# Samples' output totals three chunks behind their sums, their recurrent reads with 128 weight columns, and factors of the last stage fetched in other iterations

## The chip, the core and the metric

The kernel runs on one core of one Trainium2 chip. The metric is the device time of one execution in microseconds (us). TensorE is called PE here, its weight loads PEld, VectorE DVE, ScalarE ACT, GpSimd POOL, and the queue from which most DMAs are issued is SyncE's, SP.

## What is computed

One inference step of a decoder with two layers, for a prompt of 2048 tokens and for 8 samples of 4 tokens each (32 rows), with the same weights. Layer 0 is gated linear attention with a recurrent state (4 heads of 128 x 512), layer 1 is sliding-window attention with sinks (32 heads of 64, 4 groups). The reference, cut to what matters:

```python
def gla_mixer(h, state0, norm_g, w_in, w_gate2, b_gate, out_norm_g, w_out):
    u = rmsnorm(h, norm_g)
    q, k, v, gate, g_low = jnp.split(u @ w_in, [...], axis=-1)
    log_a = jax.nn.log_sigmoid((g_low @ w_gate2 + b_gate).astype(jnp.float32)) / A_GATE_NORMALIZER
    o, state = gla_recurrence(heads(q, A_HEAD_DK) * (A_HEAD_DK ** -0.5), heads(k, A_HEAD_DK),
                              heads(v, A_HEAD_DV), heads(log_a, A_HEAD_DK), state0)
    o = rmsnorm(o, out_norm_g).reshape(bsz, seq_len, BRANCH_WIDTH)
    return (o * jax.nn.silu(gate)) @ w_out, state
...
    # one step of the recurrence, for a chunk; b is the running sum of log_a
    out = (jnp.einsum('bhtd,bhdv->bhtv', qc * jnp.exp(b), state)
           + jnp.einsum('bhts,bhsv->bhtv', scores, vc))
    new_state = (jnp.exp(b_last[:, :, 0, :, None]) * state
                 + jnp.einsum('bhsd,bhsv->bhdv', kc * jnp.exp(b_last - b), vc))
...
hp, hs = hp + gla_mixer(hp, zeros, *w), hs + gla_mixer(hs, state_gla, *w)    # layer 0
k_p, v_p = shared_kv(hp, ...); k_n, v_n = shared_kv(hs, ...)                 # one K/V for both groups
q_p, g_p = swa_query(hp, ...); q_s, g_s = swa_query(hs, ...)                 # layer 1
hp = hp + (swa_banded(q_p, k_p, v_p, sinks) * jax.nn.silu(g_p)) @ w_out
hs = hs + (attend(q_s, cache + k_n, cache + v_n, ..., sinks) * jax.nn.silu(g_s)) @ w_out
```

## The kernel before

Each float32 operand is split into a high and a low half-precision part, and a product is made of three passes, (high, high), (high, low) and (low, high). The prompt is cut into 16 chunks of 128 rows. Program order, priorities and waits are turned into each engine's order by a scheduler; from `pin[0] = True` on (stage 3 below) PE's order is kept as it is written.

**Stage 1, the heads of layer 0** (to about 1250 us). For each of 4 heads and 4 blocks of 512 rows the kernel projects, makes scores by levels, and runs the recurrence chunk by chunk. After a head's last block the samples follow (`SampleA.steps`): `mid` makes `Sh` (scores, 96 x 32) and `qm` (tile name `qe`), the decayed queries of 32 rows, once for each of the 8 samples and zero outside that sample's 4 rows. `seq(b)` reads one sample's old state: three matmuls add `qm[:, a, b, :]` (weights, 128 x 32) times the state's halves `sh` (tile `pst`) to the bank `po` (tile `o`, 32 rows), and one matmul `kv<-ke,skn` with 96 x 128 weights makes the state's update. These are woven into the next block's work on PE.

**Stage 2, the output of layer 0** (about 1150 to 1530 us). `a_out(c)` handles chunk c: `load` fetches four transposed tiles from DRAM (`sg` or `v`, in turn, one set for odd and one for even chunks), then two halves of 48 matmuls, in the banks `pj` and `o`, two buffers each. `fin` adds the residual on DVE (`E<-pj,X` and `st<-o,X`), stores it (`hd`), and norms and transposes it for layer 1. The load of chunk c+1 stands in the program ahead of chunk c. Woven between the matmuls are steps of `prep`, which splits the weights of layer 1: `form_steps` loads four tiles of `b_w_out` (`wraw`, `qT`, `kT`), subtracts on POOL (`sth`), splits on ACT and DVE, and stores (`wf`). After chunk 7 comes the samples' output: `out_sample` runs 128 small matmuls for each half (bank `lev`, then bank `kv`; weights are the columns of `wo` and `wo1`, the moving operand is `ogTs`), and its last step, `fin`, totals on ACT and DVE (`total`, tile `ssg`), transposes on PE (`tr<-idf,ssg`), adds the residual, and after the second half norms.

**Stage 3, layer 1** (about 1530 to 2590 us). 64 blocks (4 groups of 16 chunks) and three iterations more, n from 0 to 66, TOT being 64. Iteration n projects block n (`f` steps, 24 in an iteration), makes the scores of block n-2 (`A`) and the values of block n-3 (`B`): probabilities are split (`v`), transposed by DMA (`sth<-v`, `pst<-v`), and used as weights in `kv<-rmask,sth`. In iterations 64 to 66 the `f` steps are the first products of stage 4 and the samples' output `s_out(0)`.

**Stage 4, the output of layer 1** (to the end). Two chunks (a `Pair`) are multiplied with a fast form of seven products instead of eight, `PRODS`, with factors `wf0` to `wf6`. `Pair.load` fetches transposed attention outputs (`oge`); `Pair.sums` makes on DVE and ACT the sums that are some products' other operand. For the first pair these run within stage 3: `trickle` issues loads, `summing` makes the sums, one at every sixth `f` step.

## Time and profile before

| what | us |
|---|---|
| median of 3 runs | 2882.5 |
| lowest and highest | 2880.64, 2883.82 |
| the profiled execution | 2877.55 |
| its span, first to last instruction | 2875.8 |
| PE busy (95% of the span) | 2735.2 |
| DVE, ACT, POOL busy | 1850.9, 1441.6, 1062.2 |

The profiled execution lies 4.95 us under the median, and 1.75 us of it are outside the span. Engines work side by side; a stretch of time is saved only where the engine that all others wait for is waiting or busy for nothing. A wait is put down to what ended it. A row of the timeline merges neighbours of one kind: its second number is the time from the first one's start to the last one's end, so a row's start plus the others' spacing gives the start of its last instruction.

### The profile page before, as it was taken

The numbers are of one execution on the slowest core, as the hardware profiler recorded it, in microseconds if no ns is written. First come the engines' busy times: TensorE is split into PE (matmuls) and PEld (weight loads), VectorE is DVE, ScalarE is ACT, GpSimd is POOL, SyncE is SP. The second block draws the span as 40 slices with busy tenths as digits, with TensorE's granted clock in tenths as the row PEclk, the third lists the DMA queues.
The fourth block names the chain that finished last, engine by engine and source line by source line (L and its number), as shares of the span: only waits on it lengthen the run. The fifth ranks groups of instructions, "written<-read, shape, count | busy, mean of one in ns | idle before, by whom it ended". The sixth has DMA issues, their size and how long they took to land. (4 is left out here: it accounts for less than half of the span.)

```text
span 2875.8 us, 51606 instructions
## 1 busy us (share of the span) xinstructions
PE 2735.2 (95%) x19070; PEld 1386.7 (48%) x19070; DVE 1850.9 (64%) x3815; ACT 1441.6 (50%) x3385; POOL 1062.2 (37%) x1463
## 2 busy tenths in 40 slices
PE   6899999999999999996999999999999999989999
PEld 4445444444454444443444555555555554554444
DVE  5767787677768775336412666677767766767653
ACT  6655665465546554333312555566666656641110
POOL 1242233222322321126404686666557547530000
PEclk9999999999999999998999999999999999999999
DMA  8351334124312533799976566867767788798651
GB/s 211 86 124 36 99 94 155 38 81 136 114 38 88 166 85 96 182 240 275 234 161 159 104 130 123 205 113 133 171 113 132 151 146 164 153 232 180 134 113 56
DMA packets 774230, 391.78 MB, mean 136 GB/s; under 512 B 629200, under 2 KB 698776, under 8 KB 773944
## 3 DMA queue, kind: packets, MB, share of 16 engines
q1 hardware_dynamic: 761016, 352.75, 54.4%
q0 software_dynamic: 10880, 35.66, 3.5%
q8 instruction: 149, 2.44, 0.4%
q14 instruction: 105, 0.86, 0.1%
q10 hardware_dynamic: 2080, 0.07, 0.0%
HBM read 138.90 MB, written 107.54 MB: 86 GB/s over the span
## 5 line engine op out<-in xcount | busy, mean ns | idle before, releaser
L101 PE MATMUL pj<-W,uT 128*128 128x512 f16 x5088 | 1202.0, 382 | 5.9 <-ACT qT L430 2.5
L101 PEld LDWEIGHTS <-uT 128*128 128x128 f16 x6976 | 653.3, 98 | 716.1 <-issue 42.0
L101 PE MATMUL tr<-W,uT 128*128 128x512 f16 x1536 | 365.5, 379 | 0.0
L186 POOL TENSOR_SCALAR rs_m<-ss 128x1 f32<-128x1 f32 (+3 forms) x190 | 45.7, 241 | 702.8 <-ACT og L611 246.5
L101 PEld LDWEIGHTS <-X 128*128 128x128 f16 x2744 | 185.1, 98 | 155.3 <-issue 23.4
L1273 ACT ACTIVATE o<-o,mx 128x256 f32<-128x256 f32 (+1 forms) x384 | 168.6, 439 | 181.2 <-DVE mx L1268 171.9
L1268 DVE CUSTOM_DVE_ANT_0 o<-o,madd,nsink 128x256 f32<-128x256 f32 (+1 forms) x384 | 183.8, 479 | 47.3 <-PE o L101 42.5
L101 PE MATMUL pj<-uT,W 128*128 128x512 f16 (+1 forms) x912 | 186.8, 356 | 26.8 <-DMA uT<-ogT 23.4
L198 DVE SCALAR_TENSOR_TENSOR v<-o,v 128x512 f16<-128x512 f32 (+1 forms) x192 | 128.9, 671 | 107.0 <-ACT v L197 87.1
L187 POOL TENSOR_TENSOR rs_r<-rs_m,mhalf 128x1 f32<-128x1 f32 (+2 forms) x186 | 184.5, 992 | 14.4
L101 PEld LDWEIGHTS <-W 128*128 128x128 f16 x2448 | 129.9, 99 | 112.7 <-issue 17.7
L101 PEld LDWEIGHTS <-v 128*128 128x128 f16 x976 | 94.7, 98 | 115.4 <-issue 2.6
L508 POOL TENSOR_TENSOR E<-bt 128x256 f32<-128x256 f32 x96 | 73.2, 763 | 197.6 <-DVE X L195 118.3
L195 POOL TENSOR_TENSOR ogT<-og,ogT 128x512 f16<-128x512 f32 x68 | 88.2, 1297 | 153.2 <-ACT ogT L194 148.7
L101 PEld LDWEIGHTS <-sth 128*128 128x128 f16 x2080 | 110.0, 98 | 53.8 <-DMA sth<-v 14.0
L101 PE MATMUL o<-gl,X 128*128 128x256 f16 (+1 forms) x768 | 114.6, 272 | 12.6 <-DMA X<-qe 7.2
L101 PEld LDWEIGHTS <-sg 128*128 128x128 f16 x800 | 77.8, 98 | 94.0 <-issue 1.7
L101 PE MATMUL kv<-rmask,sth 128*128 128x64 f16 x1984 | 105.7, 193 | 11.4 <-DMA sth<-v 10.5
L197 ACT ACTIVATE v<-o 128x512 f16<-128x512 f32 (+1 forms) x192 | 111.3, 580 | 10.0 <-DMA sth<-v 6.5
L1273 ACT ACTIVATE lev<-lev,mx 128x256 f32<-128x256 f32 (+1 forms) x128 | 56.5, 442 | 105.0 <-DVE mx L1268 102.9
L101 PE MATMUL kv<-rmask,pst 128*128 128x64 f16 x992 | 100.8, 193 | 7.0 <-DMA pst<-v 7.0
L195 DVE TENSOR_TENSOR X<-E,X 128x512 f16<-128x512 f32 x128 | 95.6, 747 | 13.4 <-ACT X L194 13.1
(464 smaller groups left out, 5093.6 us busy)
## 6 DMA issues: line engine op xcount, KB each, us to landing
pre<-pst POOLq DMA_DIRECT2D x72, 256.0 KB, 3.6
W<-pre SPq DMA_DIRECT2D x36, 512.0 KB, 6.8
ogd<-ogT SPq DMA_DIRECT2D x68, 256.0 KB, 2.5
wraw<-in_a_w_in_dram SPq DMA_DIRECT2D x64, 256.0 KB, 2.8
wraw<-in_b_w_in_dram SPq DMA_DIRECT2D x64, 256.0 KB, 3.6
oge<-ogT SPq DMA_DIRECT2D x64, 256.0 KB, 2.9
wraw<-in_a_w_out_dram SPq DMA_DIRECT2D x32, 256.0 KB, 3.1
X<-in_x_prompt_dram SPq DMA_DIRECT2D x32, 256.0 KB, 3.2
```

The lines of the kernel that those rows point to most:

```text
L101: return order(nc.tensor.matmul(*a, **k))
L186: pool.tensor_scalar(m[:n, :k], ss, a, b, ALU.mult, ALU.add)
L187: pool.tensor_tensor(r[:n, :k], m[:n, :k], mhalf[:n, :k], ALU.pow)
L195: eng.tensor_tensor(lo, src, hi, ALU.subtract)
L197: act(hi, src, AF.Copy, scale=sc)
L198: dve.scalar_tensor_tensor(lo, src, sc, hi, ALU.mult, ALU.subtract)
L508: pool.tensor_tensor(Ev[:, :, 0, :], ref, btv[:, :, 0, :], ALU.subtract)
L1268: dve.tensor_tensor_reduce(pm[:, z], pm[:, z], madd.rearrange("p a b -> p (a b)")[:, (2 - nk) * P :], -0.125, nsink[:, g * GRP + h : g * G ...
L1273: act(pm[:, z], pm[:, z], AF.Exp, scale=-1.0, bias=nm_[:, h : h + 1], accum_out=bx["sum"][:, h : h + 1])
```

## The change

It has three parts. (1) `out_sample`'s matmuls stay behind chunk 7, both halves in a row, and the last steps (totals, transposes, residual, norm) are called behind chunk 10; the second half's total has a tile of its own (`sqk`). (2) `Sh` becomes 96 x 128 and `qm` gets three more blocks of 32 columns, both filled with zeros by POOL; `seq(b)` reads 128 columns, blocks b to b+3, and `po` has 128 rows, of which the first 32 are used. (3) `Pair.sums` of pair 0 is ordered with its step `four` last and begins half an iteration earlier, and four fetches are called in other iterations.

```diff
--- before.py
+++ after.py
@@ -733,9 +733,10 @@
             def mid():
                 bt, S = bx["bt"], bx["S"]
                 qs, ks = self.qkv[:, 0, :], self.qkv[:, 1, :]
-                Sh = bx["Sh"] = T("Sh", [96, SMP], F16, NG)
-                act(Sh, S, AF.Copy, scale=SST / (SQ * SQ))
-                dve.scalar_tensor_tensor(Sh[32:64], S[32:64], SST / (SQ * SQ), Sh[32:64], ALU.mult, ALU.subtract)
+                Sh = bx["Sh"] = T("Sh", [96, P], F16, NG)
+                pool.memset(Sh[:, SMP:], 0.0)
+                act(Sh[:, :SMP], S, AF.Copy, scale=SST / (SQ * SQ))
+                dve.scalar_tensor_tensor(Sh[32:64, :SMP], S[32:64], SST / (SQ * SQ), Sh[32:64, :SMP], ALU.mult, ALU.subtract)
                 E0 = T("k1", [P, SMP], F32, 2)
                 act(E0, bt, AF.Exp, scale=1.0 / 16)
                 ebl = bx["ebl"] = T("ebs", [P, NS], F32, 1)
@@ -743,9 +744,10 @@
                 dve.tensor_tensor(E0, E0, qs, ALU.mult)
                 qe = T("k2", [P, 2, SMP], F16, 2)
                 split((qe[:, 0], qe[:, 1]), E0)
-                qm = bx["qm"] = T("qe", [P, 2, NS, SMP], F16, NG)
+                qm = bx["qm"] = T("qe", [P, 2, NS + 3, SMP], F16, NG)
+                pool.memset(qm[:, :, NS:], 0.0)
                 for a in range(2):
-                    dve.tensor_tensor(qm[:, a], qe[:, a].unsqueeze(1).to_broadcast([P, NS, SMP]), bmq, ALU.mult)
+                    dve.tensor_tensor(qm[:, a, :NS], qe[:, a].unsqueeze(1).to_broadcast([P, NS, SMP]), bmq, ALU.mult)
 
             def stack():
                 bt = bx["bt"]
@@ -770,7 +772,7 @@
                 vst = bx["vst"] = T("ke", [96, 512], F16, NG)
                 act(vst, pv_, AF.Copy)
                 dve.tensor_tensor(vst[64:96], pv_[64:96], vst[64:96], ALU.subtract)
-                bx["po"] = PT("o", [SMP, 512], bufs=2)
+                bx["po"] = PT("o", [P, 512], bufs=2)
                 mm(bx["po"], bx["Sh"], vst, start=True, stop=False)
 
             def seq(b):
@@ -785,7 +787,7 @@
                 sh = T("pst", [P, 2, 512], F16, 2)
                 split((sh[:, 0], sh[:, 1]), sr, SST)
                 for n, (a, z) in enumerate(PASSES):
-                    mm(bx["po"], bx["qm"][:, a, b, :], sh[:, z], start=False, stop=b == NS - 1 and n == 2)
+                    mm(bx["po"], bx["qm"][:, a, b : b + 4, :].rearrange("p b t -> p (b t)"), sh[:, z], start=False, stop=b == NS - 1 and n == 2)
                 km = T("skn", [96, P], F16, 2)
                 dve.tensor_scalar(km, bx["kst"], bm[:, b : b + 1], None, ALU.mult)
                 pkv = PT("kv", [P, 512])
@@ -798,7 +800,7 @@
                     nc.sync.dma_start(o["st_s"][0, b - 1 : b + 1, h].rearrange("b p v -> p b v"), bx["sr"])
 
             def fin():
-                po = bx["po"]
+                po = bx["po"][:SMP]
                 ob = T("pst", [SMP, 512], F32, 2)
                 ss = T("ss", [P, 3], F32, 4)
                 act(ob, po, AF.Square, accum_out=ss[:SMP, 0:1])
@@ -1085,7 +1087,7 @@
         st, total = sproj_steps(tiles, len(kts or range(16)), lambda: ogTs[0], kts, (("lev", "kv")[half], 1))
 
         def fin():
-            t = T("ssg", [P, 4, SMP], F32, 1)
+            t = T(("ssg", "sqk")[half], [P, 4, SMP], F32, 1)
             total(t, 0, 4, sc)
             pt = PT("tr", [SMP, 512], bufs=2)
             for x in range(4):
@@ -1121,8 +1123,12 @@
         aout[c + 1][0]()
         weave(aout[c][1][0] + aout[c][1][1], some(each))
         if c == 7:
-            for half, w in enumerate((wo, wo1)):
-                run(out_sample(w.cols(4), half, a_finish_s))
+            late_s = [out_sample(w.cols(4), half, a_finish_s) for half, w in enumerate((wo, wo1))]
+            for st in late_s:
+                run(st[:-1])
+        if c == 10:
+            for st in late_s:
+                st[-1]()
 
 
     def rope_mul(eng, t1, t2, src, ct, st):
@@ -1604,7 +1610,7 @@
                 put(5, z, a[1, z])
 
             if self.p == 0:
-                return [lambda f=f, z=z: f(z) for z in range(2) for f in (one, two, three, four)]
+                return [lambda f=f, z=z: f(z) for z in range(2) for f in (one, two, three)] + [lambda z=z: four(z) for z in range(2)]
             return [lambda f=f, z=z: f(z) for f in (one, two, three, four) for z in range(2)]
 
         def add(self, tag, pp, t):
@@ -1707,28 +1713,28 @@
                     trickle.pop(0)()
                 if boundary and seen == 7 and n > TOT - NCH + 3:
                     boundary.pop(0)()
-                if summing and seen % 6 == 3:
+                if summing and seen % 6 == 3 and (n > TOT or seen > 12):
                     summing.pop(0)()
             elif lists[x]:
                 lists[x].pop(0)()
         if n < NKV * NCH and c == 12:
             if g + 1 < NKV:
                 run(gw[g + 1].steps())
-        if n == TOT - 8:
+        if n == TOT - 11:
             t_ = T("uT", [P, 8, 8, P], F16, 4)
             for x in range(4):
                 pr = pairs[x // 2]
                 pr.l[x % 2] = [t_[:, 2 * x], t_[:, 2 * x + 1]]
                 pr.fetch(x % 2, pr.l[x % 2])
-        if n in (TOT - 6, TOT - 3):
-            run(quarters(wform_big, {TOT - 6: 0, TOT - 3: 2}[n]))
-        if n == TOT - 4:
+        if n in (TOT - 7, TOT - 3):
+            run(quarters(wform_big, {TOT - 7: 0, TOT - 3: 2}[n]))
+        if n == TOT - 14:
             run(quarters(wform, 3))
         if n == TOT - 1:
             trickle += [lambda x=x: pairs[0].load(x) for x in (3, 2, 0, 1)] + quarters(wform_big, 1)
+            summing += pairs[0].sums()
         if n == TOT:
             trickle += quarters(wform, 4) + quarters(wform, 5)
-            summing += pairs[0].sums()
         if n == TOT + 1:
             trickle += quarters(wform_big, 6)
         if boundary:
```

What the scheduler makes of it, as built. **PE in stage 2**, around the samples' output: `kv` is the bank of the second half's sums, `tr<-idf,ssg` and `tr<-idf,sqk` are the transposes of the totals, `W` weights. Before:

```order
L101 MATMUL kv_14338<-ogTs_3953,uT_11567 128x64
L101 LDWEIGHTS W_12641
L101 MATMUL kv_14338<-ogTs_3953,W_12641 128x32
L101 LDWEIGHTS W_12641
L101 MATMUL kv_14338<-ogTs_3953,W_12641 128x64
L104 MATMUL tr_14328<-idf,ssg_14325 32x128 x4
L101 LDWEIGHTS W_12641
L101 MATMUL kv_14338<-ogTs_3953,W_12641 128x32
L101 LDWEIGHTS W_12641
L101 MATMUL kv_14338<-ogTs_3953,W_12641 128x64
```

Now, some 730 rows further down, between chunk 10 (`sg`) and chunk 11 (`v`):

```order
L101 LDWEIGHTS sg_14638
L101 MATMUL o_14883<-W_12674,sg_14638 128x512
L104 MATMUL tr_14979<-idf,ssg_14976 32x128 x4
L104 MATMUL tr_14992<-idf,sqk_14989 32x128 x4
L101 LDWEIGHTS v_14803
L101 MATMUL pj_15029<-W_12023,v_14803 128x512
```

The transposes of both halves left the samples' sums and stand between two chunks. On SP the samples' loads and stores (`in_x_sample`, `hsd`, `uTs`) moved with them.

**DVE at the end of stage 3**, iterations 64 and 65: L1577 (L1583 in the changed file) is the first step of pair 0's sums, from the loaded `S`, `qe` and `bt`; `v<-o,v` (L198) is the low part of a block's probabilities; L1268 (L1274) is the row maximum of scores. Before:

```order
L198 SCALAR_TENSOR_TENSOR v_30932<-lev_30933,v_30931 128x512
L1315 SCALAR_TENSOR_TENSOR wraw_30992<-kv_30862,sg_30407 128x512
L1304 RECIPROCAL rv_31064<-dn_31062 128x8
L198 SCALAR_TENSOR_TENSOR v_30932<-o_30953,v_30931 128x512
L1612 SCALAR_TENSOR_TENSOR st_31010<-pj_30920,E_31007 128x512
L1268 ISA o_31018,mx_31014<-o_31018,madd,nsink 128x256
L1268 ISA mx_31014 128x1
L1577 TENSOR_TENSOR wraw_31036<-S_30834,qe_30835 128x512
```

Now:

```order
L198 SCALAR_TENSOR_TENSOR v_30949<-lev_30950,v_30948 128x512
L1618 SCALAR_TENSOR_TENSOR st_31035<-pj_30928,E_31032 128x512
L1310 RECIPROCAL rv_31084<-dn_31082 128x8
L1583 TENSOR_TENSOR wraw_30935<-S_30842,qe_30843 128x512
L1583 TENSOR_TENSOR wraw_30937<-bt_30854,bt_30855 128x512
L1321 SCALAR_TENSOR_TENSOR wraw_31009<-kv_30870,sg_30415 128x512
L198 SCALAR_TENSOR_TENSOR v_30949<-o_30970,v_30948 128x512
L1274 ISA o_31043,mx_31039<-o_31043,madd,nsink 128x256
```

Two sums moved ahead of the block's second `v`.

**SP in iterations 53 to 55** of stage 3: L1563 (L1569) fetches pair 1's tiles into `uT`, L1279 (L1285) are the transposes of probabilities. Before:

```order
L1563 DMA_TRANSPOSE uT_29222<-oge_115 128x8x128
L1230 DMA_TRANSPOSE X_28554<-qe_28551 128x8x128
L1563 DMA_TRANSPOSE uT_29222<-oge_115 128x8x128
L1279 DMA_TRANSPOSE sth_28657<-v_28572 128x8x128
L1279 DMA_TRANSPOSE pst_28659<-v_28573 128x8x128
L1214 DMA rmask_15528<-Vd_15552 128x128
```

Now:

```order
L1569 DMA_TRANSPOSE uT_28579<-oge_115 128x8x128
L1236 DMA_TRANSPOSE X_28570<-qe_28567 128x8x128
L1569 DMA_TRANSPOSE uT_28579<-oge_115 128x8x128 x3
L1285 DMA_TRANSPOSE sth_28682<-v_28597 128x8x128
L1285 DMA_TRANSPOSE pst_28684<-v_28598 128x8x128
```

Two fetches moved ahead of a block's transposes.

## Rows read from the trace of the kernel before

**Rows 1.** Windows: stretch, us, busy (count) by engine, PE clock, DMA share, GB/s.

```profile
1296.00:1368.00 72.00, 49.87 (x451) 26.99 (x450) 43.83 (x50) 27.00 (x50) 44.41 (x58) 0.83 1.06 276
```

**Rows 2.** PE's timeline, 1318 to 1372: start, us, instruction, count [idle before, releaser].

```profile
1340.58 0.55 PE L101 MATMUL kv<-ogTs,uT 128*128 128x64 f16 x9 [3.22 <-issue]
...
1360.12 1.03 PE L104 MATMUL tr<-idf,ssg 128*32 128x128 f32 x4 [18.91 <-DVE ssg L657]
1360.95 0.77 PE L101 MATMUL kv<-ogTs,W 128*128 128x32 f16 x14
...
1363.70 5.77 PE L101 MATMUL pj<-W,sg 128*128 128x512 f16 x26
```

**Rows 3.** PE's timeline, first half of chunks 10 and 11.

```profile
1405.57 10.52 PE L101 MATMUL pj<-W,sg 128*128 128x512 f16 x48
...
1426.29 10.52 PE L101 MATMUL pj<-W,v 128*128 128x512 f16 x48
```

**Rows 4.** DVE's timeline, 1341 to 1376.

```profile
1341.97 0.68 DVE L1064 SCALAR_TENSOR_TENSOR E<-pj,X 128x512 f32<-128x512 f32 x1
...
1375.95 0.41 DVE L308 TENSOR_TENSOR ss<-ss 32x1 f32<-32x1 f32 x1 [5.33 <-ACT og L307]
```

**Rows 5.** SP's timeline of DMA issues, 1370 to 1460.

```profile
1372.81 0.41 SPq L1062 DMA_DIRECT2D X<-in_x_prompt_dram  x1
1378.34 0.33 SPq L855 DMA_DIRECT2D qT<-in_b_w_out_dram  x1
...
1413.14 6.80 SPq L1057 DMA_TRANSPOSE v<-ogd  x3
```

**Rows 6.** DMA issues, 1290 to 1480: count, median us from issue to landing.

```profile
v<-ogd SPq DMA_TRANSPOSE x16, 7.0
```

**Rows 7.** PE's timeline, 378 to 384, head 1's first block.

```profile
379.24 1.68 PE L101 MATMUL pj<-W,uT 128*128 128x512 f16 x7
380.85 0.82 PE L101 MATMUL o<-pst,qe 128*32 128x512 f16 x3
381.60 0.82 PE L101 MATMUL o<-v,Sh 128*128 128x512 f16 x3
382.25 0.81 PE L101 MATMUL o<-sth,qe 128*128 128x512 f16 x3
```

**Rows 8.** Groups by form: count, busy us, mean ns, idle us before, releasers.

```profile
L101 PEld LDWEIGHTS <-uT 128*128 128x128 f16 x6976 | 653.3, 98 | 716.1 <-issue 42.0 <-DVE ssg L657 1.2
...
L101 PEld LDWEIGHTS <-qe 128*32 128x32 f16 x96 | 6.8, 94 | 15.7 <-issue 12.8
```

**Rows 9.** The same view, PE.

```profile
L101 PE MATMUL kv<-v,ke 128*128 128x512 f16 x192 | 60.8, 381 | 9.1 <-ACT v L197 5.3 <-DVE v L198 3.0 <-DMA ke<-X 0.8
```

**Rows 10.** The same view, POOL.

```profile
L1481 POOL MEMSET ogT<- 128x256 f16 x8 | 2.6, 321 | 0.0
```

**Rows 11.** PE's timeline, end of stage 3 and beginning of stage 4.

```profile
2567.09 0.23 PE L101 MATMUL kv<-rmask,sth 128*128 128x64 f16 x2 [1.24 <-DMA sth<-v]
...
2581.34 0.78 PE L101 MATMUL lev<-ogTs,uT 128*128 128x64 f16 x16 [2.90 <-DVE v L198]
...
2624.31 0.61 PE L101 MATMUL tr<-uT,ogT 128*128 128x512 f16 x1 [4.90 <-DVE ogT L195]
```

**Rows 12.** DVE's timeline, the same stretch.

```profile
2562.05 0.69 DVE L198 SCALAR_TENSOR_TENSOR v<-o,v 128x512 f16<-128x512 f32 x1
...
2565.01 0.69 DVE L1577 TENSOR_TENSOR wraw<-S,qe 128x512 f32<-128x512 f16 x1 [1.21 <-DMA qe<-oge]
...
2579.59 0.69 DVE L1620 TENSOR_TENSOR E<-E,Sh 128x512 f32<-128x512 f32 x1 [2.99 <-DMA E<-hd]
...
2621.76 1.29 DVE L1577 TENSOR_TENSOR wraw<-sth,pst 128x512 f32<-128x512 f16 x2 [5.24 <-DMA pst<-oge]
```

**Rows 13.** PE's timeline, 2403 to 2430, iterations 54 and 55.

```profile
2415.24 0.20 PE L101 MATMUL kv<-rmask,pst 128*128 128x64 f16 x1 [0.45 <-DMA pst<-v]
```

**Rows 14.** SP's timeline of DMA issues, the same stretch.

```profile
2414.11 1.30 SPq L1563 DMA_TRANSPOSE uT<-oge  x1
```

## The prediction

> **What bounds the kernel now.** I read the windows first, to find where PE is not busy, then PE's timeline there, then the timelines of DVE and SP at the same moments. PE is busy for 95% of the span, so the kernel is PE's row of work plus the places where PE stands still. The worst of all windows is the one of [rows 1]: PE works 49.9 of 72 us there, at a mean clock of 0.83, while the DMA engines are full (share 1.06). In PE's timeline [rows 2] the reader is to see one pause of 18.91 us ahead of four transposes of the samples' output total, ended by DVE's `ssg`. DVE itself was not asleep: it read chunk 7's first half only at 1341.97 [rows 4], when PE was already in the samples' sums. DVE, ACT, POOL and SP are working through the weights of layer 1 and lag behind PE by about a chunk, and the samples' total stands at the end of that line. That is the first thing the change attacks.
>
> The second thing is seen where the samples' recurrent reads are woven into other work [rows 7]. Seven matmuls with 128 weight columns start at 379.24; at a spacing of 0.216 us the last starts at 380.54 and the next should start at 380.75, but the read with 32 columns starts at 380.85. Its three end the same way: the last starts at 381.28, and the next matmul comes at 381.60 and not at 381.50. So each border between 32 and 128 columns costs PE 0.1 us. The loads themselves are as long either way, 94 and 98 ns [rows 8]; what is lost is their overlap, and the 32-column group has 12.8 us of idle time ahead of its loads that nothing explains ("issue").
>
> The third place is the end of stage 3, with short waits of PE [rows 11].
>
> **Term A, the samples' output.** The sums of both halves stay where they are; the pause of 18.91 us goes, since transposes now come three chunks (62 us, from [rows 3]) after their sums. So does the time of the four transposes that stood there, 1360.95 - 1360.12 = 0.83 us. Chunk 8 would start at 1363.70 - 18.91 - 0.83 = 1343.96. The 3.22 us of idle time before it ("issue", [rows 2]) I leave in, and with it the slow clock of the remaining sums, which the row at 1340.58 shows already (0.55 us for 9). That is 19.74 earlier. Later PE pays for eight transposes where, after this point, it had four to do: at most another 0.83. Ceiling: 18.9 us.
>
> What is late next? Chunks 8 to 11 with nothing in the way take 20.72 us each (1426.29 - 1405.57, [rows 3]), so PE would want chunk 9 at 1364.7, chunk 10 at 1385.4, and chunk 11 at 1406.1. But the tiles of chunk 11 were first issued by SP at 1413.14 [rows 5], and one takes 7.0 us to land [rows 6]. PE needs the first two at once: the second is issued 6.80 / 3 = 2.3 us later, so both are there at about 1422; before, PE came at 1426.29 and saw nothing of it. These loads stand in SP's queue behind the store of chunk 9's first half, and this behind DVE, which is paced by the loads of the weights. The change takes something out of that line: DVE's wait of 5.33 us for the samples' norm [rows 4], SP's pause of 5.1 us (1373.22 to 1378.34, [rows 5]), which has the same cause, and seven small issues of the samples on SP. The first two are one loss, 5.3; of the issues (about 5 us on SP) I count half. So chunk 11 can start at about 1422 - 8 = 1414, a gain of 12.3, or 11.5 us with the transposes. Bounds: if the line gains nothing, 1426.3 - 1422 = 4; if PE is never held up, 18.9. I take 11.5, since the removed DVE wait has a row and the rest is an estimate. That the samples' norm now sits in DVE's queue at chunk 11 costs nothing: the banks `pj` and `o` have two buffers, and the wait of 5.3 is shorter than a chunk. Without that cover it would cost 5.3.
>
> **Term B, 128 columns.** PE's timeline has 96 such reads [rows 8] in 50 separate runs over the four heads; [rows 7] shows one of them. 100 borders of 0.1 us are 10 us, the ceiling. The moving side stays at 512 columns, so the read itself is as long as before. Against it: PE also waits for other engines in these stretches (9.1 us before `kv<-v,ke`, most of it for ACT and DVE, [rows 9]), and where it comes earlier it may wait longer. I take 8.5, between 4 and 10. The eight new memsets run on POOL, the nearest row is 0.32 us each [rows 10], 2.6 in all; they write buffers that DVE's `qm` and ACT's `Sh` have waited for at the same point, and behind them on POOL stand only the level subtractions of the next block, so I take nothing; if POOL had no room, 2.6.
>
> A page speaks against this term: the Trainium skill, "TensorE: Matmul & The Clock Gate", section "LDWEIGHTS (loading the stationary operand)", says that a load's time goes with its columns, P / 1.2 ns. By it 128 columns would cost 107 ns where 32 cost 27, an estimate of 8 us more for 100 loads that nothing hides. The trace disagrees with 94 and 98 ns. The same page's section on weight-path modes says that a fast load is on with exactly 128 columns of a type that is not FP32, which agrees.
>
> **Term C, the end of stage 3.** The order shows that `wf3` and `wf0` keep their places on SP, so most of "fetched in other iterations" is no change at all. What moves is DVE: two sums now stand ahead of a block's second `v`. Their operand `qe` landed at 2565.01 [rows 12], and `v` ran at 2562.05. In its new place `v` runs after 2565.0 and two or three operations of 0.6, near 2566.9: 4.9 later. Behind it waits SP with the transposes, and behind them PE, which already waits 1.24 at 2567.09 [rows 11]; a loss of up to 4.9. On the other side, the wait of 2.99 for `hd` (2579.59, [rows 12]) leaves the path of the `v` that PE waits 2.90 us for, and the 4.90 us at 2624.31 end with DVE, which was held for 5.24 by a DMA (2621.76, [rows 12]): if PE comes late there, it waits less. So C lies between a gain of 7 and a loss of 6; I take a loss of 1, since two of the three effects cancel.
>
> **Term D, SP's queue.** Two fetches of about 1.3 us [rows 14] come ahead of a block's transposes, for which PE waits 0.45 us already (2415.24, [rows 13]): a loss of up to 2.6, and the queue is the same again some 15 us later. I take 1, between 0 and 2.6.
>
> **Sum.** 11.5 + 8.5 - 1 - 1 = 18 us of gain. The profiled execution took 2877.55, which gives 2859.55; it lies 4.95 under the median of 2882.5, so for the median I say 2864.5.
>
> **Rivals.** (1) PE is never held up by chunks 10 and 11. For it: the loads of chunk 9 are long there, and the DMA engines have idle moments. Against it: SP's times above. Then A is 18.9, the gain 25.4, the time 2857.1. Chance 0.27. (2) The pause only moves: the line behind PE gains nothing, and PE waits for chunk 10's or 11's tiles. For it: DMA share of 1.06. A is 4, the gain 10.5, the time 2872.0. Chance 0.20. (3) Slower than before, through the end of stage 3: on SP a fetch of pair 1 into a buffer that a block's transposes still read now stands ahead of the next transposes, twice; each holds the queue until they have landed, 7 us by the row of [rows 6], 14 in all, and DVE's 4.9 come on top: 18.9, and 1 from D. Against A and B at 4 and 8.5 this is 7.4 slower, 2889.9; it decides from 11.5 us at the end of stage 3 on, where A is at its lower end. Against it: the products that PE has there need nothing from SP for 20 us. Chance 0.05. (4) The change doesn't do what it says in its second part: the borders' cost comes from the change of tiles and not from the width. B is 0, the gain 9.5, the time 2873.0. For it: the loads are as long either way. Against it: from `o<-v,Sh` to `o<-sth,qe` both tiles change and the spacing stays 0.216 (381.60 and three steps are 382.25, [rows 7]). Chance 0.06. By the page's rule on columns it would be 8 us more, 2881.0; by 94 against 98 ns that has no chance beyond a small part of this 0.06.
>
> **How the numbers follow.** My forecast has 0.42. The range holds A from 4 to 18.9 with the other terms near their values, and the better and worse ends of C: 2850 to 2876. Below lies a tenth (everything at its best: 18.9 + 10 + 7 = 35.9, or 2846.6), above lies a tenth (rival 3 and the bad ends together). A measurement of this kernel tells 0.2% from no change, that is 5.8 us: faster means under 2876.7. Forecast and rival 1 are wholly there, three quarters of rivals 2 and 4: 0.42 + 0.27 + 0.15 + 0.04 = 0.88. Slower needs rival 3: 0.03; the rest, 0.09, is the same.
>
> **What would show it.** A: no pause before `tr<-idf,ssg`; chunk 8 starts some 20 us earlier against chunk 7, and what PE waits for before chunks 10 and 11 says `DMA` with `sg` or `v`; the eight transposes have no wait. B: the row of `o<-pst,qe` reads 128*128, its weight loads have no idle time of "issue", and [rows 7]' spacing is 0.216 throughout. C: the wait at `kv<-rmask,sth` grows by 3 to 5, the one at `tr<-uT,ogT` shrinks. D: 2 us before `kv<-rmask,pst` in iteration 54 or 55. I am wrong if PE's pause in stage 2 comes back whole before another chunk, if the border's 0.1 us stay, or if the end of stage 3 loses more than 6.

## The result, and the profile after

| what | before | changed |
|---|---|---|
| median of 5 runs on one chip, us | 2880.66 | 2864.75 |
| lowest and highest, us | 2879.26, 2883.82 | 2857.60, 2870.83 |
| the profiled execution, us | 2877.55 | 2857.86 |

The ratio is 0.9937, with a 95% interval from 0.9916 to 0.9958: faster by 0.63%, clear of the 0.2% that the prediction set as the bound. The gain of the medians is 15.9 us. The changed kernel's runs spread over 13 us, and its profiled execution is one of the fastest: between the two profiled executions lie 19.7 us, where the sum of the prediction said 18. Of the runs used below one is a slow one and left out of its figures, an execution of 8736.4 us of the kernel with blocks held back (the other four took 2840.58 to 2851.57).

To see where the 19.7 us come from, I take the start of the same matmul in both traces and subtract. The difference is the **lead** of the changed kernel: by so much earlier PE has come to this place. PE's order is nearly the same in both, so a lead that stays constant says that nothing happened, and each step in it has a place.

| place (time in the kernel before) | lead, us | gained in this stretch | predicted |
|---|---|---|---|
| chunk 7, ahead of the samples' sums (1311.9) | 13.07 | 13.07 | 8.5 (B) |
| chunk 12 (1447.0) | 23.03 | 9.96 | 11.5 (A) |
| late in stage 3 (2482.3) | 24.84 | 1.81 | -1 (D) |
| stage 4, steady (from 2641.3 on) | 19.69 | -5.15 | -1 (C) |

Of the 13.07, 10.4 are gained at the reads that part two widens; the rest comes from elsewhere in stage 1.

**Stage 2.** PE's timeline of the changed kernel from the samples' sums to chunk 11 (start, duration, instruction, count, in brackets the idle time before it and what ended it):

```profile
1326.47 0.47 PE L101 MATMUL kv<-ogTs,uT 128*128 128x64 f16 x11 [2.23 <-issue]
...
1329.77 2.54 PE L101 MATMUL pj<-W,sg 128*128 128x512 f16 x9
...
1374.63 0.69 PE L101 MATMUL pj<-W,sg 128*128 128x512 f16 x2 [2.83 <-DMA sg<-ogd]
1377.00 1.46 PE L101 MATMUL pj<-W,sg 128*128 128x512 f16 x3 [1.68 <-DMA sg<-ogd]
...
1399.68 0.60 PE L104 MATMUL tr<-idf,ssg 128*32 128x128 f32 x4
1400.11 0.60 PE L104 MATMUL tr<-idf,sqk 128*32 128x128 f32 x4
1402.07 0.61 PE L101 MATMUL pj<-W,v 128*128 128x512 f16 x2 [1.36 <-DMA v<-ogd]
1403.68 4.49 PE L101 MATMUL pj<-W,v 128*128 128x512 f16 x20 [1.00 <-DMA v<-ogd]
```

The pause of 18.91 us [rows 2] is gone, chunk 8 starts at 1329.77, and the eight transposes wait for nothing. In its place PE waits four times for tiles of chunks 10 and 11, 6.87 us together. Windows of the same execution (stretch, length, busy time and count of PE, PEld, DVE, ACT, POOL, granted clock, DMA share, GB/s) show a second cost:

```profile
1371.00:1383.00 12.00, 7.49 (x23) 2.58 (x22) 5.44 (x7) 3.54 (x7) 8.43 (x11) 0.72 1.15 250
1383.00:1400.00 17.00, 17.00 (x82) 7.84 (x80) 9.47 (x14) 7.41 (x14) 9.26 (x13) 1.00 0.98 259
1400.00:1407.00 7.00, 4.64 (x25) 2.06 (x23) 1.28 (x3) 0.72 (x2) 0.00 (x0) 1.00 1.00 229
```

Behind the two waits of chunk 10 the granted clock is 0.72 of full speed in the mean, that is a mixture of 2.4 and 1.2 GHz. The lead falls from 33.93 in chunk 8 to 26.61 in the second half of chunk 10: 7.32 us, of which 4.51 are waits and the other 2.8 are matmuls at the lower level. Behind the waits of 1.36 and 1.00 the clock stayed at 1.00.

SP's first issues for chunk 10 and for chunk 11:

```profile
1366.37 4.89 SPq L1059 DMA_TRANSPOSE sg<-ogd  x2
...
1393.34 7.91 SPq L1059 DMA_TRANSPOSE v<-ogd  x3
```

The changed kernel's view gives no time from issue to landing for these tiles; in the kernel before it was 7.0 us for `v` [rows 6].

**Stage 1.** PE's timeline around the reads of head 1, where [rows 7] stood:

```profile
377.27 1.68 PE L101 MATMUL pj<-W,uT 128*128 128x512 f16 x7
378.78 0.81 PE L101 MATMUL o<-pst,qe 128*128 128x512 f16 x3
379.43 0.81 PE L101 MATMUL o<-v,Sh 128*128 128x512 f16 x3
380.07 0.59 PE L101 MATMUL o<-sth,qe 128*128 128x512 f16 x2
```

Seven steps of 0.216 lead from 377.27 to 378.78, three more to 379.43, three more to 380.07: the extra time at the borders between reads and other matmuls is gone.

**The end of stage 3.** PE's timeline, where [rows 11] stood:

```profile
2540.26 0.23 PE L101 MATMUL kv<-rmask,sth 128*128 128x64 f16 x2 [0.52 <-DMA sth<-v]
...
2552.77 0.20 PE L101 MATMUL kv<-rmask,pst 128*128 128x64 f16 x1 [1.92 <-DMA pst<-v]
...
2561.66 0.59 PE L101 MATMUL pj<-uT,S 128*128 128x512 f16 x2 [2.17 <-DMA uT<-wf]
...
2582.01 0.60 PE L101 MATMUL tr<-W,X 128*128 128x512 f16 x2 [2.47 <-DVE st L1669]
...
2601.21 0.39 PE L101 MATMUL tr<-uT,ogT 128*128 128x512 f16 x1 [0.72 <-DVE ogT L195]
...
2617.58 1.01 PE L101 MATMUL o<-W,qe 128*128 128x512 f16 x2 [4.75 <-DVE st L1618]
```

The 2.90 before the samples' sums have gone and the 4.90 before `tr<-uT,ogT` shrank to 0.72, but three others took their place, 1.92, 2.17 and 2.47, and the one before `o<-W,qe`, 4.75 now, was 1.22 before:

```profile
2638.89 0.59 PE L101 MATMUL o<-W,qe 128*128 128x512 f16 x2 [1.22 <-DVE st L1612]
```

DVE's timeline shows two long waits of its own that were not there:

```profile
2572.53 0.69 DVE L1626 TENSOR_TENSOR E<-E,Sh 128x512 f32<-128x512 f32 x1 [10.29 <-DMA E<-hd]
...
2581.28 0.68 DVE L1669 TENSOR_TENSOR st<-tr,E 32x512 f32<-32x512 f32 x1 [5.53 <-DMA out_y_dram<-st]
```

DVE is through the first sums and stands still for a residual `hd`, where it waited 2.99 us before [rows 12]. SP had other things to do first (SP's timeline of issues):

```profile
2561.20 4.14 SPq L1285 DMA_TRANSPOSE sth<-v  x1
2565.39 1.30 SPq L1285 DMA_TRANSPOSE pst<-v  x1
2566.79 1.31 SPq L629 DMA_DIRECT2D oge<-ogT  x1
2568.20 0.57 SPq L1625 DMA_DIRECT2D E<-hd  x1
```

Behind the wait for `hd` DVE makes the residual and `st<-pj,E`; the samples' residual then waits 5.53 us more for a buffer of `st`, until that tile's store is through. Until it has read `tr`, the bank stays taken, and PE waits 2.47 us for it.

### The profile page after: what moved, and what is told of

It reads as the page before. It is cut to its first block, busy times and chain, and to the rows that moved or that the text cites. A ratio compares the mean times of both kernels' runs of the same rounds, so it can differ in the third digit from the quotient of the medians.

```text
span 2856.1 us, 51618 instructions
## 1 busy us (share of the span) xinstructions
PE 2727.5 (95%) x19070; PEld 1389.3 (49%) x19070; DVE 1848.5 (65%) x3815; ACT 1441.0 (50%) x3385; POOL 1065.6 (37%) x1471
## 4 chain that ended last, share of the span: by engine, by line
PE 58%; DVE 11%; DMA 10%; ACT 9%; issue 6%; POOL 4%; SPq 2%; DVEq 0%; POOLq 0%; ACTq 0%
PE pj L101 34%; PE o L101 11%; PE tr L101 8%; PE kv L101 3%; ACT o L1279 2%; DMA pre<-pst 2%; PE lev L101 1%; DVE v L198 1%; DMA pst<-v 1%; ACT v L197 1%; DMA wraw<-in_a_w_in_dram 1%; DMA uT<-ogT 1%; DVE o L1274 1%; DVE W L198 1%; POOL ogT L195 1%
## 5 line engine op out<-in xcount | busy, mean ns | idle before, releaser
L1279 ACT ACTIVATE o<-o,mx 128x256 f32<-128x256 f32 (+1 forms) x384 | 168.6, 439 | 174.9 <-DVE mx L1274 165.4
L1274 DVE CUSTOM_DVE_ANT_0 o<-o,madd,nsink 128x256 f32<-128x256 f32 (+1 forms) x384 | 183.9, 479 | 46.9 <-PE o L101 42.2
L198 DVE SCALAR_TENSOR_TENSOR v<-o,v 128x512 f16<-128x512 f32 (+1 forms) x192 | 128.9, 671 | 108.0 <-ACT v L197 87.9
L1279 ACT ACTIVATE lev<-lev,mx 128x256 f32<-128x256 f32 (+1 forms) x128 | 56.5, 441 | 104.2 <-DVE mx L1274 102.2
L101 PE MATMUL pj<-W,v 128*128 128x512 f16 x448 | 104.2, 379 | 2.4 <-DMA v<-ogd 2.4
```

Source lines behind the costliest of these rows:

```text
L101: return order(nc.tensor.matmul(*a, **k))
L198: dve.scalar_tensor_tensor(lo, src, sc, hi, ALU.mult, ALU.subtract)
L1274: dve.tensor_tensor_reduce(pm[:, z], pm[:, z], madd.rearrange("p a b -> p (a b)")[:, (2 - nk) * P :], -0.125, nsink[:, g * GRP + h : g * G ...
L1279: act(pm[:, z], pm[:, z], AF.Exp, scale=-1.0, bias=nm_[:, h : h + 1], accum_out=bx["sum"][:, h : h + 1])
```

## Experiments

All names and lines are those of the changed kernel unless said otherwise, and the diffs are cut (`...`) to the lines that tell the edit. The leads are against the profiled execution of the kernel before, as above; the whole table stands behind the last experiment.

**Each part alone, and the first two together.** Part one alone:

```diff
-            t = T("ssg", [P, 4, SMP], F32, 1)
+            t = T(("ssg", "sqk")[half], [P, 4, SMP], F32, 1)
...
-            for half, w in enumerate((wo, wo1)):
-                run(out_sample(w.cols(4), half, a_finish_s))
+            late_s = [out_sample(w.cols(4), half, a_finish_s) for half, w in enumerate((wo, wo1))]
+            for st in late_s:
+                run(st[:-1])
+        if c == 10:
+            for st in late_s:
+                st[-1]()
```

> The kernel before with the first part alone (the samples' totals behind chunk 10). Theory: the pause of 18.91 us is gone, and PE then waits for the tiles of chunks 10 and 11, as in the changed kernel, where stage 2 gained 10.0 us (from 13.07 us ahead at the samples' sums to 23.03 us ahead at chunk 12); the parts do not touch each other, so the gain is 10 and the time 2870.7. Rival, the side line gains nothing: gain 4, 2876.7. Rival, PE is held up only because the second part brought it there earlier: gain 18.9, 2861.8, and no wait before chunks 10 and 11.

Measured: 2867.1 us against 2875.82, ratio 0.9972 (0.9960 to 0.9984), 8.0 us faster. Stage 2 gains 8.61 us of lead, and PE waits 3.71, 2.66 and 1.05 us for tiles of chunks 10 and 11. So these waits come with part one and not with the earlier arrival through part two; the rival of 18.9 falls, and the ceiling is cut as the theory said.

Part two alone, that is the read below, the zeros in `Sh` and `qm`, and the bank of 128 rows:

```diff
...
-                    mm(bx["po"], bx["qm"][:, a, b, :], sh[:, z], start=False, stop=b == NS - 1 and n == 2)
+                    mm(bx["po"], bx["qm"][:, a, b : b + 4, :].rearrange("p b t -> p (b t)"), sh[:, z], start=False, stop=b == NS - 1 and n == 2)
```

> The kernel before with the second part alone (128 columns). Theory: the border's extra time is all that goes; the starts of the reads and their neighbours in the trace of before stand 8.5 us further apart in sum than at 0.216 us each, so the time is 2872.2, and PE is 8.5 us ahead at the end of stage 1. Rival: the 13.07 us by which the changed kernel is ahead there all come from this part (shorter waits of PE, too): 2867.6. Rival: the width is not the cause: 2880.7, spacings of 0.31 us as before.

Measured: 2868.6 us against 2875.82, ratio 0.9965 (0.9951 to 0.9979), 10.1 us faster. The width is the cause. Its size is best read where the reads are: over the reads of the four heads the lead grows by 2.30, 2.93, 2.76 and 2.93 us, 10.9 together (in the later kernel with blocks held back 2.31, 2.93, 2.84 and 2.93, or 11.0), and by 0.00 in parts one and three alone. The rival that this part brings all 13.07 us of lead falls with these 10.9 (at chunk 7 the lead is 7.62 here, 3.3 us having been lost elsewhere in stage 1). The weights' group by form (count, busy us, mean ns, idle us before and what ended it) has lost its unexplained idle time, with 96 loads more than before in the same group:

```profile
L101 PEld LDWEIGHTS <-qe 128*128 128x128 f16 x524 | 50.3, 98 | 59.1 <-issue 2.2
```

In the kernel before, the 96 narrow loads alone had 12.8 us of "issue" [rows 8]. In the changed kernel the same group has 0.5 us of it in stage 1.

Part three alone, the last six pieces of the diff without the others:

```diff
-                return [lambda f=f, z=z: f(z) for z in range(2) for f in (one, two, three, four)]
+                return [lambda f=f, z=z: f(z) for z in range(2) for f in (one, two, three)] + [lambda z=z: four(z) for z in range(2)]
...
-        if n == TOT - 8:
+        if n == TOT - 11:
```

> The kernel before with the third part alone (sums of pair 0 and fetches). Theory: the 5.2 us that the changed kernel loses between 2500 and 2640 us are this part's, by DVE and SP standing in another order there, and the 1.8 us that it gains before are not: 2885.9. Rival: the 5.2 us come only from PE's arriving 25 us earlier, and the part by itself does nothing or gains the 1.8: 2878.9 to 2880.7.

Measured: 2882.64 us against 2875.82, ratio 1.0019 (1.0009 to 1.0029), 5.5 us slower. From 2482 us to stage 4 the lead falls by 5.09, nearly as much as in the changed kernel (5.15), although PE comes here some 30 us later than in the changed kernel. The loss belongs to this part and not to an earlier arrival. In the middle of stage 3 it gains nothing (0.23 lost).

Parts one and two without part three:

```diff
-        if n == TOT - 11:
+        if n == TOT - 8:
...
-            summing += pairs[0].sums()
         if n == TOT:
             trickle += quarters(wform, 4) + quarters(wform, 5)
+            summing += pairs[0].sums()
```

> The changed kernel without the third part. Theory: the loss of 5.2 us at the end of stage 3 is the third part's, so this one is faster than the changed kernel by about 5 us, 2859.6 against 2864.8, and the waits at the end of stage 3 stand as in the kernel before (2.90 us before the samples' sums, 4.90 before the first product's transposes' bank). Rival: the loss comes with arriving earlier: 2864.8. Rival, the third part is a gain of 3: 2868.

Measured: 2857.07 us against 2875.82, ratio 0.9935 (0.9916 to 0.9955), 18.7 us faster; parts one and two alone make 8.0 and 10.1, so they add up. At the end of stage 3 the loss is 2.11 us instead of 5.15. Of the two waits that were to stand there as before, 4.90 stands at 4.87, but 2.90 is 1.10. By the whole times this kernel can't be told from the changed one (0.9937); the place shows the difference, the stopwatch doesn't.

**What costs at a border.** The kernel before with reads of 64 columns (`Sh`, `qm` and the bank grow to match):

```diff
...
-                    mm(bx["po"], bx["qm"][:, a, b, :], sh[:, z], start=False, stop=b == NS - 1 and n == 2)
+                    mm(bx["po"], bx["qm"][:, a, b : b + 2, :].rearrange("p b t -> p (b t)"), sh[:, z], start=False, stop=b == NS - 1 and n == 2)
```

> The kernel before with the samples' recurrent reads 64 columns wide instead of 32 (qm with one more block of 32 zero columns, Sh 96 x 64, the bank 64 rows). Theory: the border costs PE its overlap at any width under 128, so the first wide matmul after a read still starts 0.31 us later and not 0.216, and nothing is gained. Rival: the cost grows with the difference in columns: 64 columns would give about 0.28 us at a border. Rival: what matters is that the two groups differ at all, and wider loads cost more by themselves: above 0.31 us. With 128 columns the spacing was 0.216 in 96 of 96 reads.

PE's timeline, and the loads' group by form:

```profile
375.83 1.68 PE L101 MATMUL pj<-W,uT 128*128 128x512 f16 x7
377.44 0.83 PE L101 MATMUL o<-pst,qe 128*64 128x512 f16 x3
378.21 0.82 PE L101 MATMUL o<-v,Sh 128*128 128x512 f16 x3
```

```profile
L101 PEld LDWEIGHTS <-qe 128*64 128x64 f16 x96 | 8.1, 108 | 15.4 <-issue 12.8
```

Seven steps take 1.61 us where 1.51 are due: the border is 0.1 us, the median spacing into a read is 0.309 and out of it 0.312, the same as with 32 columns. The loads take 108 ns and keep the same 12.8 us of idle time. So the cost doesn't shrink with the difference in columns; of the widths tried, it is there at 32 and 64 and gone at 128. Weight columns are also rows of the bank that is written (32, 64, 128), so these runs don't separate the two. At the samples' sums this kernel stands within 0.06 us of the kernel before.

**Which half of part three.** On parts one and two, only the order and the start of the sums; then only the fetches:

```diff
-                return [lambda f=f, z=z: f(z) for z in range(2) for f in (one, two, three, four)]
+                return [lambda f=f, z=z: f(z) for z in range(2) for f in (one, two, three)] + [lambda z=z: four(z) for z in range(2)]
...
+            summing += pairs[0].sums()
         if n == TOT:
             trickle += quarters(wform, 4) + quarters(wform, 5)
-            summing += pairs[0].sums()
```

> The kernel with parts one and two, and of the third part only the order and the start of pair 0's sums. Between 2475 us (of the kernel before) and 2680 us the changed kernel loses 5.2 us against the kernel before, the third part alone 5.1, and parts one and two without the third 2.1. Theory: the sums cause it, so PE loses about 5 here too, with its waits before the products that follow DVE's residual of the samples and of the first pair. Rival: the fetches cause it: 2 here. The whole time then is about 3 us more than that of parts one and two, which were 0.65% faster than the kernel before.

Measured: ratio 0.9948 (0.9934 to 0.9962); the end of stage 3 loses 5.61 us.

```diff
-        if n == TOT - 8:
+        if n == TOT - 11:
...
-        if n in (TOT - 6, TOT - 3):
+        if n in (TOT - 7, TOT - 3):
...
-        if n == TOT - 4:
+        if n == TOT - 14:
```

> The kernel with parts one and two, and of the third part only the fetches in other iterations. Theory: the fetches do nothing at the end of stage 3 (PE loses about 2 us between 2475 and 2680 us, as without the third part), and cost at most 1 to 2 us of PE's waits between 2300 and 2475 us. Rival: they cause the loss at the end: 5. Rival, the wait for a block's transposes behind two fetches: 2.6 us before the values of a block in iterations 54 or 55.

Measured: ratio 0.9931 (0.9916 to 0.9946); the end of stage 3 loses 1.60 us, like the kernels without any of part three. It is the sums that cost there, and not the fetches. What the fetches do is seen at the place that the second rival named, iteration 54. PE's timeline of the changed kernel, then of the one with the fetches alone:

```profile
2391.96 0.23 PE L101 MATMUL kv<-rmask,sth 128*128 128x64 f16 x2 [1.02 <-DMA sth<-v]
2392.84 0.20 PE L101 MATMUL kv<-rmask,pst 128*128 128x64 f16 x1 [0.65 <-DMA pst<-v]
```

```profile
2397.44 0.20 PE L101 MATMUL kv<-rmask,pst 128*128 128x64 f16 x1 [1.10 <-DMA pst<-v]
```

Part three alone has 1.18 and 0.97 there. The kernel before has 0.45 [rows 13], and the ten others without the moved fetches have 0.38 or nothing. So the fetches cost what the theory allowed, 0.65 to 1.7 us at this place. In the sum over the middle of stage 3 this can't be seen: this kernel loses 5.56 us there, mostly through one wait of 3.82 us at 1824, before any of the fetches moved, and the changed kernel, with the same fetches, gains 1.81.

I then split the sums' change, the order alone and the earlier start alone, one execution each:

```diff
-                return [lambda f=f, z=z: f(z) for z in range(2) for f in (one, two, three, four)]
+                return [lambda f=f, z=z: f(z) for z in range(2) for f in (one, two, three)] + [lambda z=z: four(z) for z in range(2)]
```

> Parts one and two, and of the third part only the order of pair 0's sums (the step four of both halves last); the sums begin where they began. Theory: the loss at the end of stage 3 (5.6 us between 2475 and 2680 us with all of the sums' change, 2.1 without) comes from the earlier begin, which puts the sums ahead of a block's second v on DVE; here it stays near 2.1. Rival: the order alone takes the tiles st and X earlier, and the loss is here, 5.

```diff
-                if summing and seen % 6 == 3:
+                if summing and seen % 6 == 3 and (n > TOT or seen > 12):
...
+            summing += pairs[0].sums()
         if n == TOT:
             trickle += quarters(wform, 4) + quarters(wform, 5)
-            summing += pairs[0].sums()
```

> Parts one and two, and of the third part only the earlier begin of pair 0's sums, in their old order. Theory: the loss of 5.6 us between 2475 and 2680 us is here. Rival: it is the order's, and this one loses 2.1.

Measured: the order alone loses 5.61 us at the end of stage 3, the start alone 7.44, both together 5.61. The start loses as my theory said, but the order does so too, as its rival said: either half alone costs as much as both, so that neither is the one culprit. The waits stand at other places in each. The largest of PE's timeline for the order alone, and the second of the start alone (the largest is 4.18, in the table below):

```profile
2623.60 1.01 PE L101 MATMUL o<-W,qe 128*128 128x512 f16 x2 [7.97 <-ACT qe L194]
```

```profile
2569.52 1.04 PE L101 MATMUL pj<-uT,S 128*128 128x512 f16 x2 [3.95 <-DMA uT<-wf]
```

The same four places in all traces (PE's wait there in us; the nine kernels without a change to the sums are the kernel before and eight of these experiments; "both" are the changed kernel, part three alone and the run above):

| PE's wait before (time in the kernel before) | sums unchanged | order alone | start alone | both |
|---|---|---|---|---|
| `kv<-rmask,pst` (2575.9) | 0 | 0 | 3.84 | 1.92, 3.41, 3.41 |
| `tr<-W,X` (2600.7) | 0 | 0 | 0 | 2.47, 3.29, 3.24 |
| `tr<-uT,ogT` (2624.3) | 4.04 to 5.75 | 0 | 0 | 0.72, 0.90, 0 |
| `o<-W,qe` (2638.9) | 0.39 to 3.84 | 7.97 | 4.18 | 4.75, 4.40, 4.63 |

Either half of the change takes away the third wait and lengthens the fourth; the earlier start adds the first, and both halves together add the second. Each new order of pair 0's sums tried here put something else late. Why the old one fits best was not settled.

**What keeps chunks 10 and 11 waiting.** On parts one and two, the last three of the eight blocks of the factors' preparation wait for the first half of chunks 10, 11 and 12:

```diff
+                if gate is not None:
+                    pool.tensor_copy(t[:1, :1], hdone[gate][:1, :1])
                 nc.sync.dma_start(t, i["b_w_out"][0][k * P : (k + 1) * P, z * 512 : z * 512 + 512])
...
-        weave(aout[c][1][0] + aout[c][1][1], some(each))
+        weave(aout[c][1][0] + aout[c][1][1], some(each) + (form_steps(c - 6, c - 1) if c > 10 else []))
```

> The kernel with parts one and two, where the last three of the eight blocks of the last stage's factors are prepared behind chunks 10, 11 and 12: four one-element copies on POOL, from the first half of that chunk, hold each block's loads back. In parts one and two alone PE waits 3.28, 3.77, 1.48 and 0.96 us for the tiles of chunks 10 and 11. Theory: these waits come from the line of the weights' preparation ahead of the tiles on SP and on the DMA engines, and chunks 12 to 15 have room (DMA share 0.58 to 0.88 behind 1420 us): the waits go, and PE gains up to 9.5 us more, 28 us in all against the kernel before instead of 18.7. Rival: the tiles are late because they stand behind the store of the chunk before in SP's queue, whatever is prepared: the waits stay and the time is that of parts one and two, 0.65% under the kernel before. Rival: the preparation only moves the waits to chunks 12 to 15: the same time, with waits there.

Measured: ratio 0.9892 (0.9875 to 0.9909), 31 us of 2876.08; the profiled execution took 2847.79. PE's timeline from chunk 9 to chunk 11:

```profile
1350.50 10.52 PE L101 MATMUL pj<-W,v 128*128 128x512 f16 x48
...
1371.22 10.52 PE L101 MATMUL pj<-W,sg 128*128 128x512 f16 x48
...
1391.94 0.60 PE L104 MATMUL tr<-idf,ssg 128*32 128x128 f32 x4
1392.37 0.60 PE L104 MATMUL tr<-idf,sqk 128*32 128x128 f32 x4
1392.81 2.54 PE L101 MATMUL pj<-W,v 128*128 128x512 f16 x11
```

Chunks 9 and 10 take 20.72 us each, as in [rows 3], and the tiles are there. No wait appears in chunks 12 to 15 either. Stage 2 gains 20.50 us of lead, twice the changed kernel's 9.96. So the waits came from the line of the weights' preparation, and the store of the chunk before, which still stands ahead of the tiles on SP, was no obstacle by itself. Whether it was the line's place in SP's queue or its load on the DMA engines is not separated. This version beats both kernels: against the kernel before on its own chip its interval ends at 0.9909, the changed kernel's begins at 0.9916.

Does the shorter line make part one needless? Part two and the held-back blocks, with the samples' totals where they were before:

```diff
         if c == 7:
             for half, w in enumerate((wo, wo1)):
                 run(out_sample(w.cols(4), half, a_finish_s))
```

> Part two alone, and the last three of the eight blocks of the factors prepared behind chunks 10 to 12; the samples' totals stand within their sums as in the kernel before. Theory: the pause ahead of the samples' transposes stays near 19 to 20 us, since the blocks that keep DVE from the total at chunk 7 are the first five; with nothing to wait for later, the time is that of part two alone, 10 us under the kernel before. Rival: the shorter line lets DVE reach the total in time, the pause goes, and part one is not needed: some 28 us under the kernel before.

```profile
1346.48 1.03 PE L104 MATMUL tr<-idf,ssg 128*32 128x128 f32 x4 [18.19 <-DVE ssg L657]
```

Measured: one execution of 2866.06 us against one of 2878.11 for the kernel before, and PE's timeline has the pause nearly in full. The first five blocks are enough to keep DVE from the total. Without part one the held-back blocks bring little: stage 2 gains 0.93 us here, against 8.61 with part one alone and 20.50 with both.

**One chunk or three.** Parts one and two, with the last steps behind chunk 8:

```diff
-        if c == 10:
+        if c == 8:
             for st in late_s:
                 st[-1]()
```

> Parts one and two, but the samples' totals, transposes, residual and norm stand behind chunk 8, one chunk behind their sums and not three. Without the third part the second half's total was done on DVE at 1351.2 us and chunk 8 on PE at 1346.6. Theory: PE waits some 4.6 us for it ahead of the transposes behind chunk 8, and the samples' norm stands again in DVE's and SP's queues while the weights are prepared, so that the tiles of chunks 10 and 11 come up to 5 us later: at chunk 12 PE is 0 to 5 us behind the kernel with the totals behind chunk 10, which was 10.35 us ahead of the kernel before by this stretch. Rival: the pause comes back whole (18.9 us). Rival: no wait at all, one chunk is enough, and the stretch gains 10.35 as well.

```profile
1352.83 0.98 PE L104 MATMUL tr<-idf,sqk 128*32 128x128 f32 x4 [2.51 <-DVE sqk L657]
```

Measured: 2856.35 us in one execution; PE waits 2.51 us for the second half's total (4.6 were expected), and stage 2 gains 9.18 us of lead, 1.2 less than with three chunks. The wait of one place is taken off the wait at the next: before chunk 10 only 0.58 us are left, before chunk 11 2.12 and 1.38. Most of part one's gain needs one chunk of distance.

The leads, as a table. "Reads" is stage 1 to chunk 7; "stage 2" from there to chunk 12; "middle" to 2482 us; "end" from 2482 us to 2645, behind which the leads stay within 0.4 us. Positive is gained.

| kernel | reads | stage 2 | middle | end |
|---|---|---|---|---|
| changed | 13.07 | 9.96 | 1.81 | -5.15 |
| part one | 2.81 | 8.61 | 0.88 | -1.66 |
| part two | 7.62 | -1.17 | 1.34 | 0.08 |
| part three | -5.94 | 1.44 | -0.23 | -5.09 |
| parts one and two | 14.89 | 10.35 | 3.13 | -2.11 |
| 64 columns | -0.06 | 0.77 | -0.12 | -2.33 |
| one, two, sums | 10.82 | 7.90 | -1.05 | -5.61 |
| one, two, fetches | 12.85 | 10.97 | -5.56 | -1.60 |
| one, two, blocks held back | 12.98 | 20.50 | -2.08 | -1.29 |
| one, two, behind chunk 8 | 14.79 | 9.18 | -0.86 | -1.92 |
| one, two, order | 10.99 | 8.50 | -1.57 | -5.61 |
| one, two, start | 9.50 | 8.35 | -1.16 | -7.44 |
| two, blocks held back | 12.45 | 0.93 | 0.48 | -2.35 |

## Why the prediction came out right

The total, 2864.5 forecast and 2864.75 measured, agrees better than its terms do, and in this it is luck. In the leads B and D came out 4.6 and 2.8 us better than forecast, A and C 1.5 and 4.2 worse. And the kernel before took 2880.66 us in the comparison, not the 2882.5 from which I subtracted: the gain of the medians is 15.9, where 18 was forecast.

**Term A held in size and in its frame: the pause goes, and the next tiles come late.** Chunk 8 was to start 19.74 us earlier by this part. Its lead grows from 13.07 to 33.93, by 20.86; 1 us of the difference is the idle time of "issue" that I left in as 3.22 and that is 2.23 here. For what is late next I named the tiles of chunk 11, with a start of chunk 11 near 1414 in the old time; with the 13.07 added back it starts at 1415.1. The net of 9.96 lies 1.54 under 11.5, and the bounds of 4 and 18.9 enclose all eight kernels with part one and the old preparation (7.90 to 10.97). Three things inside it were wrong. PE already waits before chunk 10, for which I priced nothing, though the trace of before shows it. I wanted PE at chunk 10 at 1385.4, and SP's first issue for its tiles came only then (SP's timeline of the kernel before):

```profile
1386.05 5.19 SPq L1057 DMA_TRANSPOSE sg<-ogd  x2
```

The slow clock behind waits had no place in my sum, and costs about 3 us here. And I explained the shorter line by DVE's wait of 5.3 us for the samples' norm and seven issues on SP; with the norm back among the preparation (behind chunk 8) the first issue for chunk 11 comes only 1.0 us later (1392.34 against 1391.35, one execution each), so they seem to have been worth about 1 us and not 7.8. The line did come 6.7 us earlier in the changed kernel (1393.34 and 13.07 are 1406.4, against 1413.14 in [rows 5]); what else gave that stays open.

**Term B was right in cause and too small.** At the reads 10.4 us are gained in the changed kernel, 10.9 with part two alone and 11.0 with blocks held back, where I took 8.5 and called 10 the ceiling. Summed over the starts in the trace of before, the borders into and out of the 96 reads make 9.6 us over their due spacing, as counted; I had left out the four matmuls with `Sh` as weights, which were 32 columns wide too and have borders of their own (0.6), and 10 ns between one narrow read and the next (0.3). The discount for waiting longer where PE comes earlier was hardly due here: 0.45 us before `o<-ke,Sh` in head 1. It can be due. In four other kernels with the same reads (parts one and two; with the sums; with the order; with the totals behind chunk 8) PE waits 0.45 and 0.84 us there in heads 1 and 2 and 0.35 to 0.54 before reads, and of the gain 8.5 to 8.9 are left. The rival that the width is not the cause falls with the run of part two alone. The load's own time (94, 108, 98 ns for 32, 64, 128 columns) doesn't go with the loss; the idle time ahead of the loads does (12.8 and 12.8 us, and with 128 columns at most 0.5 in all of stage 1). Why a narrow load leaves that idle time no run shows. By the Trainium skill ("TensorE: Matmul & The Clock Gate", "LDWEIGHTS (loading the stationary operand)") the time of a load follows its columns. By that rule this part would have been a loss; the three measured durations don't follow it.

**Term C had the right places and the wrong balance.** I saw gains up to 7 and losses up to 6 and took a loss of 1. It is 5.15; over the five kernels with a change to the sums 5.09 to 7.44, over the eight without it between a gain of 0.08 and a loss of 2.35 (mean 1.6: the profiled execution before seems to have been lucky there by as much). So the sums cost about 4 us. The two gains that I expected came (2.90 and 4.90 fell to nothing and 0.72), but of the second a part comes back at `o<-W,qe`. The loss came too, one wait later than I named. The 1.24 at `kv<-rmask,sth` became 0.52: the transposes for it are on SP ahead of the moved `v`. The transposes behind the moved `v` serve the next wait. DVE's and SP's timelines of the changed kernel:

```profile
2539.62 0.68 DVE L198 SCALAR_TENSOR_TENSOR v<-o,v 128x512 f16<-128x512 f32 x1
```

```profile
2536.78 1.24 SPq L1285 DMA_TRANSPOSE sth<-v  x1
...
2542.02 1.72 SPq L1285 DMA_TRANSPOSE sth<-v  x1
...
2545.70 2.63 SPq L1285 DMA_TRANSPOSE pst<-v  x1
```

For the `pst` of 2545.70 PE waits 1.92, where it had waited for nothing: the first row of the table of four places, which is there in the four kernels with the earlier start and in no other. What I had not looked for is what DVE meets when it gets ahead: it stands 10.29 us for `hd` behind SP's transposes, and then a bank stays taken.

**Term D came at its place, and its sum can't be told.** A loss of 1 was forecast. In iteration 54, that I named, PE waits 1.02 us for `sth` and 0.65 for `pst`, where 0.45 stood [rows 13]: a loss of 1.2. Over the whole middle of stage 3 the lead varies by more than that between kernels without the moved fetches (a gain of 3.13 to a loss of 2.08).

**The rivals.** Rival 1 (never held up) is refuted for this change and describes the kernel with blocks held back: 20.50 us. Rival 2 (the pause only moves, A at 4) was right about the waits and wrong in its price: about half of the pause came back, 6.87 us as waits and about 3 as slow clock. Rival 3 (slower through stage 3) is refuted: the fetches, which were to hold up the end of stage 3 by 14 us, lose nothing there that the kernels without them don't lose, and the loss of 5 that is there belongs to the sums and is less than the 11.5 from which it would decide. Rival 4 is refuted.

## What to carry to other kernels

When a pause goes, price what is late next by the issue and landing of its data, and look for it at each following step and not only at the one that you can name; then ask what in the line ahead could be done later, since that was worth as much again here (20.5 against 10 us). Narrow weights between wide ones can cost more than wide weights padded with zeros; the spacing of starts at the border shows it, the mean duration of the loads doesn't. Where several engines are tightly fitted, moving one engine's work earlier is not a gain by default: it was a loss in each of the three ways tried, of about 4 us with the order or both, and of nearly 6 with the start alone.

## What was not expected of the hardware

The same code doesn't take the same time up to chunk 7, where parts one and three change nothing and every engine's order is the same: against the kernel before, part one alone is 2.81 us ahead there and part three alone 5.94 us behind. One reason is seen at 465 us. PE's timeline of part three alone, then of the kernel before (the same matmuls):

```profile
467.96 0.58 PE L101 MATMUL kv<-v,ke 128*128 128x512 f16 x1 [3.85 <-ACT v L197]
468.34 1.91 PE L101 MATMUL pj<-W,uT 128*128 128x512 f16 x4
```

```profile
466.45 0.38 PE L101 MATMUL kv<-v,ke 128*128 128x512 f16 x1 [1.60 <-ACT v L197]
466.67 1.02 PE L101 MATMUL pj<-W,uT 128*128 128x512 f16 x4
```

A wait of 3.85 us instead of 1.60 is followed by four matmuls in 1.91 instead of 1.02 us. The windows of part three alone have the clock at 0.85 and 0.81 there:

```profile
460.00:470.00 10.00, 6.15 (x34) 2.60 (x33) 7.65 (x18) 6.00 (x13) 2.99 (x4) 0.85 0.50 155
470.00:480.00 10.00, 10.00 (x49) 4.32 (x48) 7.40 (x14) 4.79 (x10) 4.64 (x6) 0.81 0.61 184
```

So 2.25 us more of waiting cost 5.1 us of lead. A single trace tells the size of a term only at the place of the edit; sums over a whole stage carry several microseconds of this.
